# Split weights started at a different byte offset in each group of a projection kernel

## Chip, cores and metric

One core of a Trainium2 chip runs the whole program. The metric is the device time in microseconds (us); the time before is a median over timed executions. One execution was recorded by the profiler, and all views below are of that execution.

## The reference

One decoder layer on x of 256 rows by 1024 columns, in float32. After an input RMS norm, x is multiplied by w_in (1024 x 5648); the columns are split into the queries, keys, values and gate of a block attention (mq, mk, mv, mg), those of a gated linear attention (gq, gk, gv, gg and a low-rank gate gfg) and two merge gates (ga, gb). The two branches are projected by w_proj_a and w_proj_b, mixed by the merge gates, multiplied by w_out and normed again.

```python
proj = jnp.einsum('bsd,de->bse', h, w_in[layer])
(mq, mk, mv, mgate, gq, gk, gv, ggate, gfg, ga, gb) = jnp.split(proj, split_pts, axis=-1)
...
oa = moba_attention(rotary(mq), rotary(mk), mv) * jax.nn.silu(mgate)
ya = jnp.einsum('bse,ed->bsd', oa, w_proj_a[layer])
...
ob = rms_norm(gla_chunked(qb, kb, vb, gdec)) * jax.nn.silu(ggate)
yb = jnp.einsum('bse,ed->bsd', ob, w_proj_b[layer])
merged = (jax.nn.sigmoid(ga + b_merge[layer, 0]) * ya
          + jax.nn.sigmoid(gb + b_merge[layer, 1]) * yb)
x = x + jnp.einsum('bsd,de->bse', merged, w_out[layer])
```

## The kernel before

Every large product is done with float32r operands in three matmuls: each float32 operand is split into a rounded part (`hi`, `xh`, `mh`, ...) and the rest (`lo`, `xl`, `ml`, ...), and `three` adds hi*hi, hi*lo and lo*hi into one PSUM bank. The weights come in chunks. `load_to` issues one DMA for a chunk into the ring of five `raw` buffers; `split_to` takes a buffer of the ring `hi` and one of the ring `lo` (five each), lets ScalarE (ACT) copy raw to hi (line 179) and VectorE (DVE) subtract hi from raw into lo (line 180). `prefetch` keeps the splits some four chunks ahead of the matmuls.

The chunks are gathered in groups, which run one after the other on TensorE in the order of the `group` calls: mg, gg, gqk, mq, mk, mv, gv, ga0, ga1, gb0, gb1, then pa0, pb0, pa1, pb1, and last the w_out chunks (products `po`). There are kinds of groups:
- "F" (gqk, mq, mk, ga, gb, pa, pb) and "K" (mg): the split weights are the stationary operand, 128 x 128 at a time, and 256 columns of xh or xl (oah, obh and their rests for pa, pb) are moved through. A group of 512 columns of w_in is 96 such matmuls.
- "T" (mv, gv), "G" (gg) and `po`: the other way round. 128 x 128 of xh, xl, mh or ml stand still, and 512 (or 256, 272) columns of hi or lo are moved.

The small products of the two attention branches run as generators (`start_side`), which the planner (`tick`) puts between the matmuls of the groups. The planner counts sizes, not addresses, so the order of instructions is fixed by the program. All matmuls have line 91 (helper `mm`), all transposes line 96.

Where the operands lie: each buffer of hi and lo is `SMAX` = 1088 float32 long, that is 34 times 128 bytes, so that all ten start at the same place within a block of 128 bytes, 32 bytes past its begin. Two small unused tiles, `gap0` and `gap1`, stand around xh and xl; xh, xl, mh, ml, oah, oal, obh, obl and the tiles `gs` and `sumsr` of the product `e` all start 96 bytes past the begin of such a block. All steps inside these tiles that a matmul takes are multiples of 128 bytes. "Distance" below is the start of the moving operand less that of the stationary one, within a block of 128 bytes: it is 64 bytes for every matmul of every group before. Where TensorE goes from a matmul on one pair to one whose weights are gs, mh or (after a "T" group) hi, the operand that moves and the weights that are loaded meanwhile are at distance 0.

```python
    WMAX = 1056
    SMAX = 1088
    RAW, SPLIT = 5, 5
    ...
    one.tile([P, 8], F32, name="gap0")
    xh = one.tile([P, KD, S], F32R, name="xh", tag="xh")
    xl = one.tile([P, KD, S], F32R, name="xl", tag="xl")
    one.tile([P, 24], F32, name="gap1")
```

Of the kernel before, what the change touches and what calls it, by code (L numbers as in the profile page):

```python
# [35 lines left out]
SLACK = 0.9  # L36
COMPANY, PATIENCE = 4, 4.5

C_MQ, C_MK, C_MV, C_MG = 0, 512, 1024, 1536
C_GQ, C_GV, C_GG, C_FG, C_GA, C_GB = 2048, 2560, 3072, 3584, 3600, 4624  # L40
RANK = 16
# [37 lines left out]
def layer(ctx, tc, x, norm_in_g, w_in, b_merge, w_fg2, b_fg, gla_g, w_pa, w_pb, w_out, norm_f_g,  # L79
# [19 lines left out]
    def f32(ap):  # L99
        return ap.bitcast(F32)  # L100
# [11 lines left out]
    chunks = []  # L112
    groups = []

    def group(kind, name, src, c0, n, nk, step=2):
        ids = []
        if kind == "F":
            parts = [(c0 + p, 256, k0, 4) for p in range(0, n, 256) for k0 in range(0, nk, 4)]
        else:
            parts = [(c0, n, k0, step) for k0 in range(0, nk, step)]  # L120
        for c, w, k0, k in parts:
            ids.append(len(chunks))
            chunks.append(dict(src=src, c0=c, n=w, k0=k0, nk=k))
        groups.append(dict(kind=kind, name=name, ids=ids, nk=nk))

    group("K", "mg", w_in, C_MG, 512, KD, 1)
    group("G", "gg", w_in, C_GG, 528, KD)
    group("F", "gqk", w_in, C_GQ, 512, KD)
    group("F", "mq", w_in, C_MQ, 512, KD)
    group("F", "mk", w_in, C_MK, 512, KD)  # L130
# [10 lines left out]
    for half in range(2):  # L141
        for n in range(2):
            for k in range(4 * half, 4 * half + 4, 2):
                oids[n, k // 2] = len(chunks)
                chunks.append(dict(src=w_out, c0=n * 512, n=512, k0=k, nk=2))

    WMAX = 1056
    SMAX = 1088
# [20 lines left out]
    def split_to(n):  # L169
        while done[0] < min(len(chunks), n):  # L170
            c = chunks[done[0]]
            size = c["nk"] * c["n"]
            w = c["n"]
            row = w if w % 32 == 0 else 544
            hi = ring.tile([P, SMAX], F32R, name="hi", bufs=SPLIT)
            lo = ring.tile([P, SMAX], F32R, name="lo", bufs=SPLIT)
            c["hi"], c["lo"] = (t[:, :c["nk"] * row].rearrange("p (k n) -> p k n", n=row)[:, :, :w] for t in (hi, lo))
            raw = c["raw"].rearrange("p (k n) -> p k n", n=w)
            nc.scalar.copy(c["hi"], raw)  # L179
            nc.vector.tensor_sub(c["lo"], raw, f32(c["hi"]))  # L180
            done[0] += 1

    def prefetch(i):

        load_to(i + SPLIT + RAW - 2)
        split_to(i + SPLIT - 1)
# [90 lines left out]
    for k in range(2):  # L277
        split_to(k + 1)
        x_part(k)
# [444 lines left out]
    for g in groups:  # L724
        ids, name = g["ids"], g["name"]
        if g["kind"] == "K":
            ps = [small(f"{name}{f}") for f in range(3)] + [bank(f"{name}3", "side", 1)]
            for i in ids:
                c = chunks[i]
                k = c["k0"]  # L730
                if k == 5:
                    squares(0)
                if k == 6:
                    squares(1)
                for f in range(4):
                    fs = slice(f * P, (f + 1) * P)
                    if f == 2:
                        if k + 2 < KD:
                            x_part(k + 2)
                        split_to(i + SPLIT - 1 if k > 3 else i + 3)  # L740
                    three(ps[f][:, :S], c["hi"][:, 0, fs], c["lo"][:, 0, fs], xh[:, k, :], xl[:, k, :],
                          k == 0, k == KD - 1)
            start_side(gates_mg(ps))
        elif g["kind"] == "G":
            ps = {(t, b): (small if t and b else bank)(f"{name}{t}{b}") for t in range(NT) for b in range(2)}
            for i in ids:
                prefetch(i)
                c = chunks[i]
                for kk in range(c["nk"]):
                    k = c["k0"] + kk  # L750
# [8 lines left out]
        elif g["kind"] == "T":  # L759
            ps = [bank(f"{name}{t}") for t in range(NT)]  # L760
            for i in ids:
                prefetch(i)
                c = chunks[i]
                for kk in range(c["nk"]):
                    k = c["k0"] + kk
# [6 lines left out]
        elif g["kind"] == "F":  # L772
            src = {"pa": (oah, oal), "pb": (obh, obl)}.get(name[:2], (xh, xl))
# [18 lines left out]
            nk = g["nk"]  # L792
            per = nk // 4
            for b in range(len(ids) // per):
# [6 lines left out]
                for j in range(2):  # L801
# [3 lines left out]
                    for k in range(nk):  # L805
                        c = chunks[i + k // 4]
# [94 lines left out]
```

## Time and profile before

| | |
|---|---|
| time, median of 3 runs | 211.7 us (210.26 to 211.94) |
| the profiled execution's own time | 209.73 us |
| its span, first to last instruction | 208.0 us |
| granted TensorE clock, mean | 0.997 |
| TensorE matmul (PE) busy | 198.8 us, 96% |
| TensorE weight load (PEld) busy | 182.4 us, 88% |
| VectorE (DVE) busy | 141.6 us, 68% |
| ScalarE (ACT) busy | 122.6 us, 59% |

Matmuls overlap in the pipeline, so that the recorded duration of one (276 ns, say) is longer than the time to the start of the next. What counts is this time from start to start, called the interval or the pace below. It is read from the starts in the timeline or from a run of matmuls in the chain of work, as length over count.

### The profile page before, as it was taken

The page shows a single profiled execution, that of the slowest core. Times are in us where ns is not written, and L with a number is a line of the kernel's source. Part 1 is how long each engine was busy: PE and PEld are TensorE (multiplying, and loading weights), DVE is VectorE, ACT ScalarE, POOL GpSimd, SP SyncE. Part 2 cuts the span into 40 slices and gives each one's busy share as a digit, 9 for nine tenths or more (in the row PEclk, how much of TensorE's full clock was granted, in tenths as well). Part 3 has the DMA queues.
Part 4 walks back from the last instruction along what each step waited for, and adds up shares of the span by engine and source line. Part 5 has one row for each costly group of instructions (what it writes and reads, how often), then busy time and mean ns, then how long its engine had stood idle before and what let it go on. Part 6 is the DMA issues. An engine that isn't in the chain of part 4 may idle for free.

```text
span 208.0 us, 4231 instructions
## 1 busy us (share of the span) xinstructions
PE 198.8 (96%) x1683; PEld 182.4 (88%) x1683; DVE 141.6 (68%) x261; ACT 122.6 (59%) x205; POOL 32.5 (16%) x31
## 2 busy tenths in 40 slices
PE   7999999999999999998999999999999999999970
PEld 2899999899999988775789999999999999989870
DVE  1566778969545899989765556945393959755371
ACT  4369927871999984156775629846455554552251
POOL 2000025800214540103000000200010060420011
PEclk9999999999999999999999999999999999999998
DMA  5999896594364456660343563966344584600022
GB/s 144 349 379 323 238 310 211 135 296 149 101 199 117 145 158 191 193 218 14 107 123 86 182 193 114 294 210 198 108 151 154 168 301 135 204 4 2 0 101 101
DMA packets 28501, 35.39 MB, mean 170 GB/s; under 512 B 1305, under 2 KB 21442, under 8 KB 28482
## 3 DMA queue, kind: packets, MB, share of 16 engines
q1 hardware_dynamic: 28178, 34.60, 54.1%
q10 hardware_dynamic: 304, 0.53, 0.7%
q8 instruction: 13, 0.21, 0.4%
q14 instruction: 6, 0.05, 0.1%
HBM read 34.08 MB, written 1.05 MB: 169 GB/s over the span
## 4 chain that ended last, share of the span: by engine, by line
PE 67%; DVE 11%; ACT 11%; issue 5%; DMA 2%; SPq 1%; POOLq 0%; POOL 0%; ACTq 0%; DVEq 0%
PE ga L91 11%; PE gb L91 11%; PE po L91 8%; PE gg L91 6%; PE gqk L91 6%; PE pa L91 5%; PE pb L91 5%; DVE lo L180 4%; ACT hi L179 4%; PE mg L91 3%; ACT z L700 3%; PE mq L91 3%; DMA xt<-in_x_dram 2%; PE gv L91 2%; DVE EX L417 2%
## 5 line engine op out<-in xcount | busy, mean ns | idle before, releaser
L180 DVE TENSOR_TENSOR lo<-raw,hi 128x1024 fp32r<-128x1024 f32 (+1 forms) x56 | 70.4, 1269 | 23.5 <-ACT hi L179 23.5
L179 ACT CAST hi<-raw 128x1024 fp32r<-128x1024 f32 (+1 forms) x56 | 57.7, 1048 | 21.5 <-PE po L91 6.0
L91 PE MATMUL ga<-xh,hi 128*128 128x256 f32 x64 | 18.1, 283 | 0.0
L91 PE MATMUL gb<-xh,hi 128*128 128x256 f32 x64 | 18.1, 282 | 0.0
L91 PE MATMUL gb<-xh,lo 128*128 128x256 f32 x64 | 17.9, 279 | 0.0
L91 PE MATMUL gb<-xl,hi 128*128 128x256 f32 x64 | 17.9, 279 | 0.0
L91 PE MATMUL ga<-xh,lo 128*128 128x256 f32 x64 | 17.8, 278 | 0.0
L91 PE MATMUL ga<-xl,hi 128*128 128x256 f32 x64 | 17.8, 278 | 0.0
L91 PE MATMUL po<-hi,ml 128*128 128x512 f32 (+1 forms) x40 | 13.9, 347 | 0.0
L91 PE MATMUL po<-lo,mh 128*128 128x512 f32 (+1 forms) x40 | 13.8, 346 | 0.0
L91 PE MATMUL po<-hi,mh 128*128 128x512 f32 (+1 forms) x40 | 13.7, 343 | 0.0
L91 PEld LDWEIGHTS ga<-xh,hi 128*128 128x128 f32 x64 | 12.1, 189 | 0.5 <-issue 0.5
L558 ACT ACTIVATE sm<-sm,mx 128x128 f32<-128x128 f32 (+1 forms) x16 | 7.1, 444 | 8.7 <-DVE mx L553 8.6
L91 PEld LDWEIGHTS gb<-xh,lo 128*128 128x128 f32 x64 | 12.1, 189 | 0.0
L91 PEld LDWEIGHTS gb<-xh,hi 128*128 128x128 f32 x64 | 12.1, 189 | 0.0
L91 PEld LDWEIGHTS ga<-xl,hi 128*128 128x128 f32 x64 | 12.0, 188 | 0.0
L91 PEld LDWEIGHTS gb<-xl,hi 128*128 128x128 f32 x64 | 12.0, 188 | 0.0
L91 PEld LDWEIGHTS ga<-xh,lo 128*128 128x128 f32 x64 | 12.0, 188 | 0.0
L511 POOL TENSOR_TENSOR s<-s,mhalf 128x4 f32<-128x4 f32 x2 | 2.3, 1172 | 54.6 <-DVE s L510 54.6
L624 POOL TENSOR_TENSOR m<-m,sa 128x512 f32<-128x512 f32 x4 | 7.0, 1743 | 23.9 <-DVE m L622 22.0
L91 PE MATMUL mg<-xh,hi 128*128 128x256 f32 x32 | 10.3, 321 | 0.0
L91 PE MATMUL mg<-xl,hi 128*128 128x256 f32 x32 | 9.5, 296 | 0.0
(197 smaller groups left out, 605.7 us busy)
## 6 DMA issues: line engine op xcount, KB each, us to landing
raw<-in_w_in_dram SPq DMA_DIRECT2D x36, 512.0 KB, 3.7
raw<-in_w_out_dram SPq DMA_DIRECT2D x8, 512.0 KB, 4.8
raw<-in_w_in_dram SPq DMA_DIRECT2D x4, 528.0 KB, 6.0
first<-in_w_in_dram SPq DMA_DIRECT2D x8, 256.0 KB, 5.5
raw<-in_w_proj_a_dram SPq DMA_DIRECT2D x4, 512.0 KB, 3.5
raw<-in_w_proj_b_dram SPq DMA_DIRECT2D x4, 512.0 KB, 4.4
xt<-in_x_dram SPq DMA_DIRECT2D x3, 256.0 KB, 5.7
late<-in_norm_f_g_dram SPq DMA_DIRECT2D x1, 512.0 KB, 5.0
```

The lines of the kernel that those rows point to most:

```text
L91: nc.tensor.matmul(out, lhsT, rhs, start=start, stop=stop)
L179: nc.scalar.copy(c["hi"], raw)
L180: nc.vector.tensor_sub(c["lo"], raw, f32(c["hi"]))
L417: nc.vector.tensor_mul(e, e, halves(src, LEVELS[l], which))
L511: nc.gpsimd.tensor_tensor(s4, s4, mhalf, op=OP.pow)
L558: nc.scalar.activation(sm[i][:, cs], sm[i][:, cs], AF.Exp, bias=mx[:, i, t:t + 1], scale=0.125, accum_out=den[:, i, t:t + 1])
L624: nc.gpsimd.tensor_add(m, m, cut(sg["ga"]))
L700: nc.scalar.copy(z[i:i + 32], p2[i ^ 32:(i ^ 32) + 32])
```

## The change

Each chunk gets a `shift`, in float32 elements, by its group; hi and lo of the chunk start so many elements later in their ring buffers. The buffers, their sizes and places, and all instructions and waits stay as they are; only start addresses differ. Groups that the table does not name (pa, pb) have 0, as have mg and gg.

```diff
+SHIFT = {'mg': 0, 'gg': 0, 'gqk': 4, 'mq': 12, 'mk': 28, 'mv': 16, 'gv': 8, 'ga0': 24, 'ga1': 20, 'gb0': 30, 'gb1': 2}
...
-            chunks.append(dict(src=src, c0=c, n=w, k0=k0, nk=k))
+            chunks.append(dict(src=src, c0=c, n=w, k0=k0, nk=k, shift=SHIFT.get(name, 0)))
...
-                chunks.append(dict(src=w_out, c0=n * 512, n=512, k0=k, nk=2))
+                chunks.append(dict(src=w_out, c0=n * 512, n=512, k0=k, nk=2, shift=(4, 28)[n]))
...
-            c["hi"], c["lo"] = (t[:, :c["nk"] * row].rearrange("p (k n) -> p k n", n=row)[:, :, :w] for t in (hi, lo))
+            c["hi"], c["lo"] = (t[:, c["shift"]:c["shift"] + c["nk"] * row].rearrange("p (k n) -> p k n", n=row)[:, :, :w] for t in (hi, lo))
```

In bytes, the distance goes from 64 to: gqk 48, mq 16, mk 80, ga0 96, ga1 112, gb0 72, gb1 56 (weights shifted), mv 0, gv 96, po 80 for its first 512 columns and 48 for the others (moving data shifted). mg, gg, pa and pb stay at 64. The shifts of gb0 and gb1 (120 and 8 bytes) are no multiples of 16 bytes; all others are.

## Rows read from the trace of the kernel before

**Rows 1.** The page's parts 1 and 2: busy time and share of the engines, and in 40 equal slices of the span the busy tenths of TensorE and its granted clock.

```profile
PE 198.8 (96%) x1683; PEld 182.4 (88%) x1683; DVE 141.6 (68%) x261; ACT 122.6 (59%) x205; POOL 32.5 (16%) x31
...
PE   7999999999999999998999999999999999999970
...
PEclk9999999999999999999999999999999999999998
```

**Rows 2.** Busy time by stretch: the stretch, its length, busy us and instructions of each engine, granted clock, DMA share, GB/s. The stretches are gqk, mq with mk, ga, and po.

```profile
32.00:44.50 12.50, 12.50 (x102) 11.94 (x101) 11.47 (x17) 9.45 (x13) 6.94 (x3) 1.00 0.63 178
44.50:69.00 24.50, 24.50 (x203) 24.20 (x202) 14.50 (x18) 19.89 (x29) 4.30 (x2) 1.00 0.57 171
...
102.50:131.50 29.00, 29.00 (x249) 26.80 (x248) 17.97 (x38) 18.31 (x32) 1.33 (x1) 1.00 0.47 135
...
178.40:200.00 21.60, 21.60 (x120) 18.64 (x119) 11.72 (x17) 7.52 (x11) 4.01 (x3) 1.00 0.12 39
```

**Rows 3.** The chain of work that ended last, in order of time: start us, length us, what. Its runs of TensorE in gqk, mq, ga, gb, pa, pb and po.

```profile
33.38 2.83 PE gqk L91 x24
...
36.43 2.83 PE gqk L91 x24
...
40.31 5.85 PE gqk L91 x48
46.16 5.67 PE mq L91 x48
...
107.26 7.02 PE ga L91 x60
...
116.53 7.50 PE ga L91 x66
...
125.72 7.26 PE ga L91 x60
132.99 5.66 PE gb L91 x48
...
139.08 7.51 PE gb L91 x66
...
148.38 9.19 PE gb L91 x78
...
163.46 5.44 PE pb L91 x48
```

**Rows 4.** Instructions by tile: the matmuls of one pair of operands, their number, the recorded duration of one in ns (least/median/most), and the start of the first and the last in us.

```profile
L91 PE MATMUL mq<-xh,hi x32: 280/281/281, 46.0 to 57.6; 128*128 128x256 f32 x32
...
L91 PE MATMUL ga<-xh,hi x64: 276/276/384, 103.9 to 132.5; 128*128 128x256 f32 x64
...
L91 PE MATMUL gb<-xh,hi x64: 276/281/365, 132.8 to 157.0; 128*128 128x256 f32 x64
...
L91 PE MATMUL pb<-obh,hi x32: 276/276/276, 163.3 to 179.3; 128*128 128x256 f32 x32
```

**Rows 5.** The same chain of work where it leaves TensorE in mq, two of its pieces on ACT and DVE, and where it comes back in gv.

```profile
51.85 0.58 ACT z L700
...
54.23 1.05 ACT hi L179
...
75.11 1.21 DVE lo L180
...
78.78 1.14 DVE lo L180
...
95.94 0.92 PE sc L91 x4
96.86 3.64 PE gv L91 x15
```

**Rows 6.** Waits of TensorE: who waited for whom, us in total, times, longest us.

```profile
PE pt L96 <- DVE AT L463: 0.6, 1, 0.6
PE sc L91 <- DVE mx L551: 0.2, 1, 0.2
```

**Rows 7.** Timeline of TensorE in mk, where one product e stands between two matmuls of mk: start us, duration us, line, what.

```profile
60.22 0.28 PE L91 MATMUL mk<-xh,lo 128*128 128x256 f32 x1
60.34 0.39 PE L91 MATMUL e<-sumsr,gs 128*128 128x512 f32 x1
60.56 0.28 PE L91 MATMUL mk<-xh,hi 128*128 128x256 f32 x1
```

**Rows 8.** The same view in gv and then po, moving 512 columns: the first and the last of 14 matmuls without another between, and two neighbours of po behind the last matmul of pb.

```profile
97.13 0.39 PE L91 MATMUL gv<-lo,xh 128*128 128x512 f32 x1
...
100.10 0.40 PE L91 MATMUL gv<-hi,xl 128*128 128x512 f32 x1
...
179.51 0.28 PE L91 MATMUL pb<-obh,lo 128*128 128x256 f32 x1
179.62 0.39 PE L91 MATMUL po<-hi,mh 128*128 128x512 f32 x1
179.85 0.39 PE L91 MATMUL po<-lo,mh 128*128 128x512 f32 x1
```

**Rows 9.** The chain again, a pair of transposes of 128 columns between the matmuls of mg.

```profile
10.13 0.22 PE xp L96 x2
```

**Rows 10.** The weight loads (PEld) by tile, in mq and in pb; columns as in rows 4.

```profile
L91 PEld LDWEIGHTS mq<-xh,hi x32: 187/188/188, 45.9 to 57.5; 128*128 128x128 f32 x32
...
L91 PEld LDWEIGHTS mq<-xh,lo x32: 192/192/192, 46.1 to 57.8; 128*128 128x128 f32 x32
...
L91 PEld LDWEIGHTS pb<-obh,lo x32: 187/188/188, 163.4 to 179.4; 128*128 128x128 f32 x32
```

**Rows 11.** The two halves of the split by source line: number, duration of one in ns (least/median/most), start of the first and the last, forms.

```profile
L179 ACT CAST hi<-raw x56: 1029/1049/1073, 18.4 to 190.1; 128x1024 fp32r<-128x1024 f32 x52, 128x1056 fp32r<-128x1056 f32 x4
...
L180 DVE TENSOR_TENSOR lo<-raw,hi x56: 1207/1218/2309, 19.5 to 191.2; 128x1024 fp32r<-128x1024 f32 x52, 128x1056 fp32r<-128x1056 f32 x4
```

## Prediction

> **What bounds the kernel now.** I read the page's first two parts, then the stretches, then the chain, then single instructions. TensorE is busy for 96% of the span and its granted clock is at the higher level, 2.4 GHz, in every slice [rows 1]; in gqk, mq, mk, ga and po it is busy for the whole stretch at a granted clock of 1.00 [rows 2]. A share of busy time does not tell whether TensorE goes at its best pace, so I read the pace from the chain: length over count.
>
> There are two paces for the same kind of matmul (256 columns moved). pb takes 5.44 us for 48, 113.3 ns each; mq 5.67 for 48, 118.1; gqk 2.83 for 24, 117.9 [rows 3]. ga and gb have both: 7.50 for 66 (113.6) in ga, 7.26 for 60 behind it (121, the re-start after an inserted product included), 5.66 for 48 in gb (117.9), then 7.51 for 66 (113.8), then 9.19 for 78 (117.8) [rows 3]. The recorded durations say it without an inserted product: 276 ns all through pb, 281 all through mq, and in gb a least of 276 with a median of 281 [rows 4]. The reader is to see that the operands of ga and gb lie at the same distance of 64 bytes throughout, and still go at either pace; it changes at an inserted product and then holds for dozens of matmuls. In the slow pace one of the three weight loads takes 192 ns in place of 188 [rows 10]. So the distance, which is all that this change alters, does not by itself set the pace; what it could do is decide which of the two paces the two read streams of TensorE fall into, or open a third.
>
> TensorE does not set the end everywhere. From 51.85 us the chain runs over ACT and DVE (the z copies, splits, the factors) and comes back to TensorE at 95.94 [rows 5]; TensorE waits 0.6 and 0.2 us for DVE near its end [rows 6]. Up to that place a faster mq (second half), mk, mv or gv only lengthens these waits, and a slower one is covered up to 0.6 + 0.2 = 0.8 us.
>
> **The change part by part.** Nothing is added, removed or moved: same instructions, waits, transfers and buffers, and the planner counts sizes. Four terms can differ.
>
> First, the matmuls of 256 columns. On the chain and shifted are gqk (96), the first half of mq (48), ga (192) and gb (192), 528 in all. At the slow pace are gqk 96, mq 48, ga 60 and gb 48 + 78 [rows 3], 330; the other 198 I count as fast (in the run of 60 at 107.26, 117 each, some near its begin are slow). One matmul changing pace is worth 117.8 - 113.3 = 4.5 ns. All 330 to fast: 330 x 4.5 = 1.5 us less. All 198 to slow: 0.9 us more.
>
> Second, the 512-column products. gv has 13 intervals from 97.13 to 100.10, 228 ns each [rows 8]; po goes 0.23 from start to start [rows 8]. The shortest 512-column interval in the rows is that of e, 0.22 (0.215 to 0.225 with the rounding) [rows 7]. On the path are 72 of po and some 20 of gv behind 96.86: from 92 x (228 - 220) = 0.7 us less to the same amount more; I take 0, since the rows show one pace only.
>
> Third, what a distance other than 64 costs. The trace has no lasting run at one. Its nearest rows are single matmuls during which weights at distance 0 are loaded: mk before e, 0.12 us (0.115 to 0.125) [rows 7], where its neighbours take 0.118, and the last of pb before po, 0.11 (0.105 to 0.115) [rows 8], where its neighbours take 0.113. So distance 0 is worth between -8 and +7 ns beside its neighbours and most likely nothing; below zero too, since no row excludes a gain. I take 0 and keep +7 for the range.
>
> Fourth, ACT and DVE write hi and lo at new starts. Their durations lie between 1029 and 1073 ns for hi and at a median of 1218, least 1207, for lo, over two row pitches [rows 11]. Where TensorE is the bound they are covered: one chunk lasts 24 matmuls, 24 x 0.113 = 2.7 us, against 1.2 of DVE. Without cover they stand in the stretch from 51.85 to 95.94, where lo varies from 1.14 to 1.21 [rows 5]; with a dozen splits there, 12 x 0.07 = 0.8 us either way. I take 0: the starts differ, the sizes do not.
>
> The sum. In ga and gb the pace is now dealt about evenly (186 of 384 slow). I expect the new starts to deal it anew at each inserted product, without a lasting cost. Dealt evenly, gqk and mq go from 144 slow to 72: 72 x 4.5 = 0.3 us less; ga and gb keep their share. Against its own time the profiled execution would go from 209.73 to 209.4. The median of the runs shown is 211.7, 2.0 above that execution, and carries the same difference: **211.4 us**. Timed runs of this kernel spread over 0.8%, so about 1% is what a measurement can tell from no change.
>
> The Trainium skill speaks against any effect: "SBUF — State Buffer", section "Who interferes with whom", gives TensorE two independent read ports, one for the moving operand and one for weight loads, and says that TensorE never waits on anyone. By that rule the sum would be 0 and the time 211.7. The trace does not quite agree: with 256 columns at one granted clock there are intervals of 113.3 and 117.8 ns with nothing between the matmuls, and a load of 192 in place of 188 in the slow ones, so something on TensorE's read side does give way.
>
> **The rivals.**
>
> *The slow pace needs 64 bytes.* If other distances cannot hold it, all 330 go fast: -1.5 us, and po and gv gain up to 0.3 with it, some -1.8, 209.9 us. For it: pa and pb, on other tiles, show the slow pace nowhere to speak of. Against it: those too lie at 64.
>
> *The floor falls.* 113.3 ns is the shortest lasting interval of a 256-column matmul here. Two transposes take 0.22 us, 110 ns each [rows 9]. If a better distance brings the shifted 528 there, 330 x 7.8 + 198 x 3.3 = 3.2 us less, 208.5. Against it: no row of a float32r matmul is under 113. The Trainium skill, "TensorE: Matmul & The Clock Gate", section "Back-to-back issue gap", would give 256 / 2.4 + 2.5 = 109 ns, an estimate from that page which lies near the transposes and which no 256-column float32r row reaches.
>
> *A lasting collision (the slower case).* Moving and weight reads meet again and again at some of the distances, as they may in the single matmul before e, and never slip apart. Its place is gqk, ga and gb, where TensorE has no cover, and it decides as soon as the interval stays above 117.8. At 121.4 ns, half way between the slow pace and the upper bound of 0.125 from that row: 330 x 3.6 + 198 x 8.1 = 2.8 us more, 214.5; at 0.125 throughout 330 x 7.2 + 198 x 11.7 = 4.7 us, 216.4. In mq's second half, mk, mv and gv it would hide in the 0.8 us. For it: each shifted group gets another distance, and only 64 is known to be harmless. Against it: distance 0 before po costs nothing that the row shows.
>
> *Lines of weights cut in gb.* gb0 and gb1 start 8 bytes off a multiple of 16. If the 512 bytes of a load's row are read in pieces of 16, it takes 33 pieces in place of 32, and its 188 ns [rows 10] grow by up to 6, and 192 matmuls cost 1.1 us: 212.5. In the Trainium skill it is the page "SBUF — State Buffer", section "Door 1: The DMA port swizzle", that gives 16 bytes as the line whose crossing costs; no row here shows such a load.
>
> **How the numbers follow.** Forecast (dealt anew, or no effect at all): 0.50. Slow pace gone: 0.20. Floor falls: 0.06. Collision: 0.19. Cut lines alone: 0.05. Low end of the range: the fastest run shown, 210.26, less the 1.5 of the second case, 208.8. High end: the slowest, 211.94, plus the 2.8 of the collision, 214.7. Left out are the floor case and the dearer half of the collisions, under 2 in 10. Faster by over 1% (below 209.6): the floor case and half of the second, which ends close to that bound, 0.16. Slower by over 1% (above 213.8): most of the collision, 0.16 with a share of the others. The same: 0.68.
>
> **What would show it.** The pace is read again by tile and by chain. Forecast: medians of 276 and 281 ns only, mixed in gqk, mq, mk, ga and gb; 188 and 192 in the loads; mg, gg, pa, pb as before until the first shifted group. Second case: 276 from gqk to gb1 and the waits before 96 us longer by about the gain of mk, mv and gv. Collision: a third duration above 281 in some groups and not in others, the same in a group's whole length. Cut lines: loads above 192 in gb alone. DVE and ACT durations of lines 179 and 180 unchanged. The prediction is wrong if a lasting interval appears below 113 or above 125 ns, or if the splits' own durations move by more than 0.07 us.

## The result and the profile after

Before and after were timed side by side: 209.79 us before, 211.84 us after (medians of 18 runs each). The difference of the medians is 2.05 us. The recorded ratio, over the fast executions alone, is 1.0088, with a 95% interval of 1.0066 to 1.0110: the change costs 1.85 us, or 1.4 to 2.3. The forecast was 0.3 us less. The time lies inside the stated range, the direction was wrong.

The page after, engines and granted clock; it answers to [rows 1]. This view does not tell what happened: TensorE is busy for the same 96% and the clock is at its upper level as before.

```profile
PE 200.6 (96%) x1683; PEld 183.7 (88%) x1683; DVE 141.6 (68%) x261; ACT 122.6 (59%) x205; POOL 38.2 (18%) x31
...
PE   6999999999999999989999999999999999999980
...
PEclk9999999999999999999999999999999999999996
```

The chain of work after (start us, length us, what), the same runs of matmuls as in [rows 3]:

```profile
32.70 2.85 PE gqk L93 x24
...
35.76 2.85 PE gqk L93 x24
...
39.66 5.89 PE gqk L93 x48
...
95.44 0.92 PE sc L93 x4
...
106.86 7.39 PE ga L93 x60
...
116.50 7.91 PE ga L93 x66
...
126.10 7.39 PE ga L93 x60
133.49 5.66 PE gb L93 x48
...
139.59 7.80 PE gb L93 x66
...
149.17 9.23 PE gb L93 x78
...
164.31 5.44 PE pb L93 x48
...
180.63 16.77 PE po L93 x84
```

po in the same view of the kernel before:

```profile
179.78 16.47 PE po L91 x84
```

Piece by piece against [rows 3]: ga went from 7.02 + 7.50 + 7.26 to 7.39 + 7.91 + 7.39, 0.91 us more. gb went from 5.66 + 7.51 + 9.19 to 5.66 + 7.80 + 9.23, 0.33 more. pb, which is not shifted, stayed at 5.44. The first 84 matmuls of po took 16.47 us before and 16.77 after, and its other 36 some 0.17 more (from the starts). The stretches that were slow before (ga's last, gb's first and last) lost 0 to 0.13 us; the ones that were fast lost 0.3 to 0.4 each. From the first gqk piece to the sc matmuls at the place where the chain comes back to TensorE [rows 5] the time went from 62.56 (33.38 to 95.94) to 62.74 (32.70 to 95.44), 0.18 more. From sc to the first long piece of ga, gv's last matmuls among them, it went from 11.32 (95.94 to 107.26) to 11.42, 0.10 more. Sum: 0.18 + 0.10 + 0.91 + 0.33 + 0.30 + 0.17 = 1.99 us between these two executions, inside the 1.4 to 2.3 of the timed runs. (The span itself grew by 1.3 us only, since the first gqk piece, behind unshifted work alone, starts 0.7 us earlier in this execution.)

By tile, least/median/most duration in ns, after; it answers to [rows 4]:

```profile
L93 PE MATMUL mq<-xh,hi x32: 277/283/289, 45.4 to 57.2; 128*128 128x256 f32 x32
...
L93 PE MATMUL ga<-xh,hi x64: 278/284/389, 103.5 to 133.0; 128*128 128x256 f32 x64
...
L93 PE MATMUL gb<-xh,hi x64: 277/278/368, 133.3 to 157.9; 128*128 128x256 f32 x64
...
L93 PE MATMUL pb<-obh,hi x32: 276/276/276, 164.1 to 180.1; 128*128 128x256 f32 x32
```

Before there were two values, 276 and 281. Now the shifted groups hold neither: apart from matmuls right behind an inserted product (the 389 and 368) the durations spread from 277 to 289, and no pair in ga or gb goes down to 276. pb is at 276 throughout, as before.

The splits are as they were [rows 11]: hi at a median of 1048 ns, lo at 1221.

```profile
L181 ACT CAST hi<-raw x56: 1031/1048/1077, 17.7 to 191.1; 128x1024 fp32r<-128x1024 f32 x52, 128x1056 fp32r<-128x1056 f32 x4
...
L182 DVE TENSOR_TENSOR lo<-raw,hi x56: 1212/1221/2325, 18.8 to 192.2; 128x1024 fp32r<-128x1024 f32 x52, 128x1056 fp32r<-128x1056 f32 x4
```

### The profile page after: what moved, and what is told of

Its sections match the earlier page's. It is cut to its first block, busy times and chain, and to the rows that moved or that the text cites. A ratio compares the mean times of both kernels' runs of the same rounds, so it can differ in the third digit from the quotient of the medians.

```text
span 209.3 us, 4231 instructions
## 1 busy us (share of the span) xinstructions
PE 200.6 (96%) x1683; PEld 183.7 (88%) x1683; DVE 141.6 (68%) x261; ACT 122.6 (59%) x205; POOL 38.2 (18%) x31
## 4 chain that ended last, share of the span: by engine, by line
PE 70%; DVE 11%; DMA 7%; issue 5%; ACT 3%; SPq 1%; POOLq 0%; POOL 0%; DVEq 0%
PE ga L93 11%; PE gb L93 11%; PE po L93 8%; PE gg L93 6%; PE gqk L93 6%; PE mq L93 5%; PE pa L93 5%; PE pb L93 5%; DMA raw<-in_w_in_dram 5%; DVE lo L182 3%; PE mk L93 3%; PE gv L93 2%; DMA first<-in_w_in_dram 2%; DVE EX L419 2%; DVE AT L465 2%
## 5 line engine op out<-in xcount | busy, mean ns | idle before, releaser
L706 POOL TENSOR_TENSOR kT<-kT,z 128x512 f32<-128x512 f32 x2 | 10.5, 5236 | 7.2 <-DVE z L705 7.2
```

The lines of the kernel that those rows point to most:

```text
L706: nc.gpsimd.tensor_add(dst, dst, z)
```

## Experiments

All experiments are the kernel before with another table of shifts, unless their diff says otherwise. "Pace" is the length of a piece of the chain over its count.

### Two parts of the change alone

```diff
-SHIFT = {'mg': 0, 'gg': 0, 'gqk': 4, 'mq': 12, 'mk': 28, 'mv': 16, 'gv': 8, 'ga0': 24, 'ga1': 20, 'gb0': 30, 'gb1': 2}
+SHIFT = {'gqk': 4, 'mq': 12, 'mk': 28, 'mv': 16, 'gv': 8}
...
-                chunks.append(dict(src=w_out, c0=n * 512, n=512, k0=k, nk=2, shift=(4, 28)[n]))
+                chunks.append(dict(src=w_out, c0=n * 512, n=512, k0=k, nk=2, shift=(0, 0)[n]))
```

> The shifts of the change in gqk, mq, mk, mv and gv alone; ga, gb and po as before. Their intervals grow by some 1 to 2 ns of 118 and 3 to 4 ns of 229, 0.6 us if all of it reached the end. Theory 'covered' (up to 96 us the end is set over ScalarE and VectorE): 0.1 to 0.3 us slower, TensorE's waits for VectorE near 95 us shorter than 0.8. Rival 'all of it counts': 0.6 us slower. Rival 'the pace lasts': the paces of ga and gb (unshifted, distance 64) change too, because they are entered from gv in another state; then up to 0.8 us either way on top.

Measured: 210.31 us against 209.79, ratio 1.0019 (0.9988 to 1.0051).

```diff
-SHIFT = {'mg': 0, 'gg': 0, 'gqk': 4, 'mq': 12, 'mk': 28, 'mv': 16, 'gv': 8, 'ga0': 24, 'ga1': 20, 'gb0': 30, 'gb1': 2}
+SHIFT = {'ga0': 24, 'ga1': 20, 'gb0': 30, 'gb1': 2}
```

> The shifts of the change in ga, gb and po alone; all groups before them as before. Theory 'distance' (no shifted group can hold the fast pace): ga and gb together 1.2 us longer, po 0.4 us longer, 1.6 to 1.8 us slower in all, nearly the whole of the change's loss. Rival 'the loss lies in the early groups': under 0.8 us slower.

Measured: 211.43 us against 209.79, ratio 1.0073 (1.0048 to 1.0098), 1.5 us of the 1.85, a little under the 1.6 to 1.8 expected. Most of the loss lies in ga, gb and po; in this trace ga and gb are 1.23 us longer, as expected. In the first of the two runs the trace shows ga and gb at the lengths of before, to 0.01 us, so the paces of the late groups do not hang on the early ones. Its piece from gqk to sc takes 62.72 us (32.85 to 95.57), 0.16 more than before, although its 256-column intervals grew by up to 2 ns for 288 matmuls (1 in gqk, 2 in mq, under 1 in mk) and its 512-column ones by 3 to 4 for 96, some 0.7 us in all. TensorE's waits for VectorE near 95 us went from 0.6 + 0.2 [rows 6] to 0.5 + 0.2 us:

```profile
PE pt L98 <- DVE AT L465: 0.5, 1, 0.5
...
PE sc L93 <- DVE mx L553: 0.2, 1, 0.2
```

The interval of the timed ratio holds both the 0.2 us of "covered" and the 0.6 us of "all of it counts". The trace speaks for the first: what arrives at the sc matmuls is 0.16 us.

### A map of distances in pa and pb

These 192 matmuls run without inserted products and were all at 113.3 ns, so each of the four pieces of 48 shows one distance without another product between. Each kernel was executed once; what is read from it is the pace of the pieces, and its time (211.33, 213.13 and 210.30 us) is not used. The three kernels differ in one line:

```diff
+SHIFT = {'pa0': 16, 'pb0': 32, 'pa1': 48, 'pb1': 0}
```

> The kernel before, with only pa and pb shifted: pa0 by 16 elements (64 bytes, distance 0), pb0 by 32 (128 bytes, distance 64 again), pa1 by 48 (192 bytes, distance 0), pb1 by 0 (distance 64). These 192 matmuls run without inserted products and all went at 113.3 ns before (5.44 us for 48). Theory 'distance' (the fast pace can be held only at a distance of 64 bytes within 128): pb0 and pb1 stay at 113.3 ns, recorded duration 276; pa0 and pa1 settle at 118 to 121 ns (5.65 to 5.8 us for 48), 0.5 us longer in all. Theory 'dealt anew' (my forecast: the distance plays no part, each start of a run falls into one of the two paces by chance): each of the four at 113.3 or at 117.8, none at another value, with no order by distance. Theory 'any shift' (the start of the weights itself, not the distance): pb0 slow as well.

```diff
+SHIFT = {'pa0': 1, 'pb0': 63, 'pa1': 2, 'pb1': 62}
```

> As map_a, with shifts of 1 element (4 bytes, distance 60) in pa0, 63 (252 bytes, distance 68) in pb0, 2 (8 bytes, distance 56) in pa1 and 62 (distance 72) in pb1. Theory 'distance': if the place that holds the fast pace is a wide one (tens of bytes), all four stay at 113.3; if it is a single place, all four go to 117.8 or a little above, 48 x 4.5 = 0.2 us each. Theory 'dealt anew': 113.3 or 117.8 without order. Theory 'cut lines' (weights that start off a multiple of 16 bytes need one more access): all four above their neighbours in loads, over 192 ns, since all four are off such a multiple.

```diff
+SHIFT = {'pa0': 8, 'pb0': 40, 'pa1': 56, 'pb1': 60}
```

> As map_a, with shifts of 8 elements (32 bytes, distance 32) in pa0, 40 (160 bytes, distance 32) in pb0, 56 (224 bytes, distance 96) in pa1 and 60 (240 bytes, distance 80) in pb1. Theory 'distance': all four above 117, the two at distance 32 alike, 96 at 120 as ga0 shows after the change, 80 at 118 as mk shows. Theory 'dealt anew': 113.3 or 117.8 without order.

The chain of the first:

```profile
158.40 5.70 PE pa L93 x48
164.09 5.66 PE pb L93 x48
169.75 5.76 PE pa L93 x48
175.51 5.65 PE pb L93 x48
```

of the second:

```profile
160.22 5.68 PE pa L93 x48
165.91 5.74 PE pb L93 x48
171.64 5.68 PE pa L93 x48
177.32 5.66 PE pb L93 x48
```

and of the third:

```profile
157.57 5.63 PE pa L93 x48
163.20 5.61 PE pb L93 x48
168.80 5.69 PE pa L93 x48
174.49 5.66 PE pb L93 x48
```

Not one of the twelve pieces is at 5.44. Divided by 48:

| distance, bytes within 128 | ns per matmul |
|---|---|
| 0 | 119 (pa0), 120 (pa1) |
| 32 | 117 (pa0, shift 8), 117 (pb0, shift 40) |
| 56 | 118 |
| 60 | 118 |
| 64, by a shift of 128 bytes | 118 |
| 64, no shift (pb1) | 118 |
| 68 | 120 |
| 72 | 118 |
| 80 | 118 |
| 96 | 119 |

In no piece off 64 bytes is the fast pace left, not even 4 bytes away (60 and 68). So far this is the theory "distance", and against "dealt anew": there are values between and above 113.3 and 117.8, and 113.3 is missing. But both pieces at 64 bytes went at 117.8 too, one of them with no shift at all. That is a miss of "distance" alone, and "any shift" does not explain pb1, which has none. What the two have in common is that the piece before them went at a distance off 64. Two expected values were missed by little: 96 bytes gave 119 and not 120, and one piece at 32 bytes went at 116.9, just under 117. "Cut lines" failed as well: off 16 bytes single loads go up to 195 ns in the second kernel, but the medians are 188 and 189, and the pieces off 16 bytes (118, 120, 118, 118) are not slower than those on it.

The same finding limits the table. Only pa0 of each kernel (0, 60 and 32 bytes) is entered as in the kernel before; every other piece stands behind one off 64, and behind such a piece even 64 bytes gave 117.8. For 32 and 96 bytes the first long piece of ga closes the gap: it goes at 113.3 ns in the kernel before, at 120 with the late shifts alone (distance 96), and at 116.7 in a later experiment (distance 32). That 56, 68, 72 and 80 bytes could not hold 113.3 after another entry is not shown. They are no copy of the slow pace, though: at 64 bytes its single intervals are 117 to 119 ns, at 56, 72 and 80 they spread over 114 to 122, 113 to 122 and 116 to 120 with nearly the same mean.

### The same distance at other addresses

```diff
+SHIFT = {'mg': 8, 'gqk': 8, 'mq': 8, 'mk': 8, 'mv': 8, 'gv': 8, 'ga0': 8, 'ga1': 8, 'gb0': 8, 'gb1': 8}
...
+                chunks.append(dict(src=w_out, c0=n * 512, n=512, k0=k, nk=2, shift=(8, 8)[n]))
...
-    one.tile([P, 8], F32, name="gap0")
+    one.tile([P, 16], F32, name="gap0")
...
-    one.tile([P, 24], F32, name="gap1")
+    one.tile([P, 16], F32, name="gap1")
```

> All split weights except those of gg, pa and pb shifted by 8 elements (32 bytes), and xh, xl, mh, ml moved by 32 bytes as well, by another split of the two unused tiles around them: every one of these matmuls has other addresses than before, and the distance of 64 bytes of before; gg goes to a distance of 32, pa and pb are untouched. Theory 'distance': paces as before, 113.3 and 117.8 both present in ga and gb, no third value there, time within 0.3% of before with a part of it for gg (96 matmuls, up to 0.3 us). Theory 'any shift' (it is the start of weights or moving data in itself that counts): gqk to po like the kernel after, some 1.8 us slower. Theory 'dealt anew': 113.3 and 117.8 present, shares unlike those of before by chance.

Measured: 209.68 us against 209.78, ratio 0.9982 (0.9949 to 1.0015). Weights and moving data both moved by 32 bytes cost nothing that can be measured, whereas pa0 with its weights alone moved by 32 bytes went from 113.3 to 117. For the pace itself it is the distance and not the address. gg, whose distance went from 64 to 32, took the same 8.85 us for its run of 71 matmuls as before, so that the price of a distance, read here from matmuls with moved xh, oah or obh, does not hold for every stream. The tiles' durations show the two values of before and only these, but in other places:

```profile
L93 PE MATMUL mq<-xh,hi x32: 276/276/282, 46.2 to 57.5; 128*128 128x256 f32 x32
```

mq goes at 276 here, at 281 before [rows 4]; so do gqk and mk. In gb the second stretch, fast before, is slow, and the last, slow before, is fast. Which of the two paces a stretch gets is thus not settled by the distance within its own products; gqk here runs behind a group off 64 bytes (gg) and is fast, where before it ran behind one at 64 and was slow. gqk to sc takes 62.00 us (33.97 to 95.97) in place of 62.56. With 288 matmuls in gqk, mq and mk at 4.5 ns less, 1.3 us less would be possible; 0.56 arrives. That is the cover of the prediction seen from the other side: gains behind the first half of mq are lost.

### Does the order inside a triple decide the pace?

```diff
-        mm(o, ah, bh, start=first, stop=False)
-        mm(o, ah, bl, start=False, stop=False)
+        mm(o, ah, bl, start=first, stop=False)
+        mm(o, ah, bh, start=False, stop=False)
```

> No shift at all; in each triple of matmuls the second and the first change places (hi with xl, then hi with xh, then lo with xh). Same matmuls, same distance of 64 bytes everywhere, another order. Theory 'entry' (at 64 bytes both paces hold, and the state in which a run is entered decides): only 113.3 and 117.8 ns occur, but in other groups than before; time anywhere from 1.5 us faster to 0.9 us slower. Rival 'fixed by tile' (something of the groups' own tiles, not the entry, decides): gqk, mq, mk slow and pa, pb fast as before, time within 0.2%.

Measured: 209.88 us against 209.79, ratio 1.0009 (0.9977 to 1.0041).

```diff
-        mm(o, ah, bh, start=first, stop=False)
-        mm(o, ah, bl, start=False, stop=False)
-        mm(o, al, bh, start=False, stop=last)
+        mm(o, al, bh, start=first, stop=False)
+        mm(o, ah, bh, start=False, stop=False)
+        mm(o, ah, bl, start=False, stop=last)
```

> No shift at all; in each triple the matmul of lo comes first (lo with xh, hi with xh, hi with xl). Expectations as for order_a: 'entry' gives 113.3 and 117.8 ns alone, in other places than before, from 1.5 us faster to 0.9 us slower; 'fixed by tile' gives the places of before and no change of time.

Measured: 209.43 us, ratio 0.9986 (0.9955 to 1.0017). In both, each stretch of ga, gb, pa and pb has the pace of before, and gqk to mk too: the chain of the second gives 7.02, 7.50 and 7.26 us in ga, 5.66, 7.51 and 9.19 in gb, the very lengths of [rows 3]. The order in a triple decides nothing, and in ga and gb the deal is no dice: in all ten traces of kernels that leave these two groups where they were (before, the early shifts alone, the map, both orders, and the kernels below with an added transpose and with shifts of 128 bytes) the same stretches are fast and the same are slow.

### A transpose as the last inserted matmul

```diff
+        if hp == HP - 1:
+            yield from take("small")
         yield from together(2)
         pair = hp // 2
...
+        if hp == HP - 1:
+            transpose(small("kick")[:, :P], ident, ident)
+            give("small")
         give("sm", 2)
...
-            yield from take("small")
+            yield from take("small", 1 + t)
             yield from together()
             o = small("o")
...
+            if t:
+                transpose(small("kick")[:, :P], ident, ident)
+                give("small")
             sq = work.tile([P, 512], F32, name="sq", tag="t512", bufs=4)
```

> No shift. One transpose of 128 columns whose result nobody reads is added behind the inserted pv product before the last stretch of ga, and one behind the last o product in gb; after these two places the kernel before runs at 117.8 ns for 108 and 78 matmuls, while it falls into 113.3 after the inserted products that end on transposes in ga, gb and pa. Theory 'entry' (at 64 bytes the state in which a run is entered decides, and a transpose as the last inserted matmul leads into the fast pace): both stretches at 113.3 ns, 186 x 4.5 ns = 0.8 us less, the two transposes 0.2 us more, 0.6 us faster in all. If the entry counts but the transpose is not what decides: one or both stretches stay at 117.8, up to 0.2 us slower. Rival 'fixed by place': both stay slow.

Measured: 209.92 us against 209.63, ratio 1.0005 (0.9980 to 1.0030). The chain of this kernel:

```profile
126.20 0.26 PE kick L98
126.46 7.07 PE ga L93 x60
133.53 5.66 PE gb L93 x48
...
148.91 0.11 PE kick L98
149.02 9.19 PE gb L93 x78
```

Both stretches stayed at 117.8. A transpose as the last matmul before a stretch does not decide.

The group mg, at 64 bytes, says the same and more. Its pieces of 12 each stand behind a pair of transposes, and this kernel changes nothing in it or ahead of it. Its second piece of 12, before and in this kernel:

```profile
10.35 1.38 PE mg L91 x12
...
10.84 1.42 PE mg L93 x12
```

From the starts, the second piece settles at 113.3 ns before and at 117.8 here, the fourth the other way round (117.8 and 113.3). Same instructions, same addresses, another deal: in mg neither the program nor the tile fixes it. What differs between the two executions is how the piece ahead went: the first piece of 12 settles at 113 ns before and runs at some 210 here (granted clock 1.00 in both). Whether the like decides in ga and gb is not shown.

### A distance that is entered twice, and what it leaves behind

```diff
+SHIFT = {'ga0': 40, 'ga1': 40, 'gb0': 40, 'gb1': 40}
```

> ga and gb alone shifted, all by 40 elements (160 bytes, distance 32), the distance at which pb0 gave the lowest interval off 64 bytes, 116.7 ns. 'A distance off 64 has one narrow band of intervals however it is entered': all of ga and gb at 116 to 118.5 after each inserted product, with neither 113.3 nor a second lasting value; ga and gb together 0.4 us longer than before (they were at 113.3 and 117.8 about evenly). 'Entry counts there as well': one stretch at 113.3, or stretches apart by more than 2 ns.

The chain of this kernel in ga, gb, pa and pb:

```profile
108.91 7.20 PE ga L93 x60
...
118.36 7.70 PE ga L93 x66
...
127.75 7.20 PE ga L93 x60
134.95 5.60 PE gb L93 x48
...
140.99 7.71 PE gb L93 x66
...
150.48 9.11 PE gb L93 x78
...
160.02 5.66 PE pa L93 x48
165.68 5.65 PE pb L93 x48
171.33 5.65 PE pa L93 x48
176.99 5.66 PE pb L93 x48
```

ga and gb sum to 44.52 us against 44.14 before, 0.38 more, as expected: every piece has a mean of 116.7 once the re-start behind an inserted product is over, whichever way it is entered. pa and pb are the second result. Nothing of theirs is changed, the transposes before them are the same, and they go at 117.8 in place of 113.3, all 192 (in the kernel with po alone shifted, executed beside this one, they are at 113.3). So 'fixed by tile' falls too: at 64 bytes both paces hold, and what ran before, even on the far side of inserted transposes, decides between them. But a group off 64 bytes does not always leave the slow pace behind it: in the kernel after the change gb ends at distance 56, and pa and pb behind it hold 113.3 (5.44 us for pb in its chain above); with the late shifts alone it is the same. po, unshifted too, shows both of its own values in this run: the first 36 matmuls of 512 columns at 233 ns from start to start and the 256-column ones behind them at 117.8, the next 36 at 229 and the last 256-column ones at 113.4 (worked out from the starts); its durations reach from 276 (256 columns) over a median of 388 to 401:

```profile
L93 PE MATMUL po<-hi,mh x40: 276/388/401, 182.5 to 204.3; 128*128 128x512 f32 x24, 128*128 128x256 f32 x16
```

The single execution took 212.86 us, 3.2 above that of the kernel before beside it; its first gqk piece starts at 35.02, 1.6 us later than in [rows 3], behind unshifted work alone, and the rest is the 0.4 of ga and gb and some 1 us of pa, pb and po in the slow pace.

### 128 bytes further

```diff
+SHIFT = {'pa0': 32, 'pb0': 32, 'pa1': 32, 'pb1': 32}
...
+                chunks.append(dict(src=w_out, c0=n * 512, n=512, k0=k, nk=2, shift=(32, 32)[n]))
```

> pa, pb and po shifted by 32 elements (128 bytes): the distance within 128 bytes stays 64, within 256 bytes it changes from 192 to 64 in pa and pb and from 64 to 192 in po. All else as before. Theory 'distance within 128': pa and pb at 113.3 as before (they are entered in the same way), po at 226 to 232, mean 229, time within 0.2% of before. Rival 'distance within 256': pa and pb at 117.8 or another value above 113.3 (192 x 4.5 ns = 0.9 us slower), po's 512-column intervals changed, perhaps to 226.7. Rival 'any shift': pa and pb at 117 to 120.

Measured: 209.77 us against 209.63, ratio 1.0015 (0.9983 to 1.0047). pa and pb hold the fast pace:

```profile
157.28 5.45 PE pa L93 x48
162.72 5.44 PE pb L93 x48
168.16 5.44 PE pa L93 x48
173.60 5.44 PE pb L93 x48
```

So for them it is 64 bytes within 128 that counts, not within 256. po went at 233 and, for 256 columns, at 117.8 ns in place of 229 and 113.3. To tell its entry from its distance, po alone:

```diff
+SHIFT = {}
...
+                chunks.append(dict(src=w_out, c0=n * 512, n=512, k0=k, nk=2, shift=(32, 32)[n]))
```

> Only po shifted, by 32 elements (128 bytes); pa and pb before it untouched, so po is entered from the fast pace as in the kernel before. In the run with pa, pb and po shifted by 128 bytes po went at 231 to 236 ns for 512 columns and 117.8 for 256, in place of 229 and 113.3. 'Entry': po back at 226 to 232, mean 229, and 113.3. 'Distance within 256 bytes' (for moved hi and lo): mean near 233 and 117.8 again, po 0.5 us longer.

```profile
L93 PE MATMUL po<-hi,mh x40: 281/393/398, 179.6 to 201.7; 128*128 128x512 f32 x24, 128*128 128x256 f32 x16
```

Again 233 and 117.8: the least duration, that of 256 columns, is 281. po is 0.5 us longer, and the one execution took 210.20 us against 209.64. By the expectation that is "within 256 bytes". But 233 and 117.8 are also the values that the unshifted po fell into behind ga and gb at distance 32. The single intervals tell the 512-column streams apart: there they repeat 233, 233, 234, here 236, 230, 236, 231, with nearly the same mean. So this is not the stream that po had there; why the means agree, and whether po could hold 229 at this shift after another entry, stays open.

No run is measurably faster than the kernel before; the best, 0.9982 and 0.9986, hold 1 in their intervals.

## Why the prediction was wrong

**The bound** was read rightly: TensorE sets the end in ga, gb and po, where 1.5 of the 1.85 us arose, and between 52 and 96 us ACT and DVE cover it (0.16 us arrives in the early part alone, 0.56 of a possible 1.3 in the run with the same distance).

**The first term** had the right two paces and the right price, 4.5 ns. The step that failed is the one behind it: "I expect the new starts to deal it anew at each inserted product, without a lasting cost." The deal was not made anew between two paces. At none of the eleven other distances tried (0 to 112) does a stream of 256-column matmuls show the fast pace, and at those of the change its place is taken by paces of 117.8 to 120 ns: the fast stretches of ga went to 120, that of gb to 118. The 198 matmuls counted as fast lost about 4.5 to 6.7 ns each, and no stretch at 117.8 ns gained.

**The third term** is where that is to be seen in the sum. I took 0 for a lasting distance other than 64, from single matmuls at distance 0 between others at 64 [rows 7, 8]. They were no guide: the last of pb before po cost nothing, a whole piece at distance 0 costs 5 to 7 ns per matmul (5.70 and 5.76 us in place of 5.44). One matmul does not show what a stream settles into. The bound of 7 ns above the neighbours held: the longest lasting interval is 120, 6.7 above the fast pace and 2.2 above the slow one.

**The second term**: po went from 229 to 231 and 232 ns (worked out from the starts), its 256-column part, 48 matmuls that neither the first nor the second term counted, from 113.3 to 119; 0.47 us in place of 0.

**The fourth term** was right: the splits' medians moved by 1 to 3 ns, inside the 0.07 us allowed.

**The rivals.** "A lasting collision", given 0.19, comes nearest: the interval off 64 bytes stays longer for whole stretches. It was priced at 121.4 ns everywhere, 2.8 us; the stretches settled at 117.8 to 120, which makes some 2 us in the traces and 1.85 timed. That moving and weight reads meet is not shown; the runs show the longer intervals only. Its sign in the profile, a duration above 281 in shifted groups alone, is there as a median (283 and 284 in mq and ga), but not "the same in a group's whole length": the durations spread. "Cut lines" fell: gb, the group off 16 bytes, lost least, and its loads stay within 192 ns, where ga's go up to 193. "The slow pace needs 64 bytes" was the wrong way round: of the distances tried it is the fast one that was found at 64 alone. "The floor falls": the shortest lasting interval of a 256-column matmul in all runs is still 113.3. The rule on independent ports, taken from the Trainium skill, "SBUF — State Buffer", section "Who interferes with whom", would have made the change cost nothing; the measured 1.85 us, and pa0's 117 in place of 113.3 with weights alone moved by 32 bytes, go against it for these matmuls.

**Luck.** The forecast of 211.4 us stands only 0.4 from the measured 211.84, but that is no merit: the three runs at hand gave 211.7 for the kernel before, the eighteen beside the change 209.79. A base 1.9 us too high and a change of the wrong sign nearly cancel.

The same views could have told more. pa and pb hold 113.3 for 192 matmuls, ga and gb flip between two exact values that then hold. That these are two ways in which two read streams fall into step is a reading that no row shows; but a change of start addresses could lose the better one, and there was no room for a gain below 113.3 in any row of a 256-column product. Dealing chances evenly among new places overlooked that the only place known to hold 113.3 ns was the distance given up.

**What stays open.** Which feature of the entry decides between 113.3 and 117.8 at 64 bytes: neither the order in a triple nor a last transpose does, a group off 64 bytes before it has led into either, and in mg the deal changes from execution to execution. Why po goes at 233 at a shift of 128 bytes. Whether 56, 68, 72 and 80 bytes (and 16, 48 and 112 of the change) could hold 113.3 after another entry. And why the intervals are longer off 64 bytes: no row shows what gives way.

## What to carry to other kernels

Read the pace of a matmul stream from start to start, and look whether it locks onto exact values; a value that holds over dozens of matmuls is no noise, and a layout change can take it away. Where the stationary and moving operands of a float32r product like these (128 x 128 weights, 256 columns) lie at 64 bytes from each other within 128, keep them there. Measure any other place in a stretch without inserted products before it goes into the kernel, one place per run: with four places in one run, 48 matmuls each, the pace of a piece also hung on the piece before it, and an untouched pb1 went at 117.8 in place of 113.3. A single instruction under another condition is no estimate for a stream under it.

## What the hardware showed that was not expected

- For 128 x 128 weights and 256 moved columns of float32r at a granted clock of 1.00, 113.3 ns from start to start occurred, of the twelve distances tried, at 64 bytes alone; at 60 and 68 bytes it was already 118 and 120, at 0 119 to 120, at 32 117. (68 was entered behind a piece at 60 only.)
- At 64 bytes a second pace of 117.8 ns is as lasting as the first, and what ran before decides which: pa and pb, untouched, ran all 192 matmuls in it after ga and gb at distance 32, though transposes stand between, and all at 113.3 after gb at 72 and 56.
- In ga and gb the deal between the two is the same in kernels that differ elsewhere: their pieces came out at 7.02, 7.50, 7.26, 5.66, 7.51 and 9.19 us, to 0.01, with the triples in two orders and before the change. It is another one when weights and moving data both move by 32 bytes, and in mg it differs between executions of the same instructions.
